# Four attention chains per step, keys paired with forget gates, and a later turn of the first HGRN queries

## The chip, the core and the metric

The kernel runs on one core of a Trainium2 chip. The metric is the device time of one execution in microseconds (us); lower is better. The program uses five engines, each with its own queue that is worked off in order: TensorE (PE in the profile, its weight loads PEld), VectorE (DVE), ScalarE (ACT), GpSimd (POOL) and SyncE (SP, which only issues DMAs). They wait for each other through semaphores.

## The reference, cut to what matters

One layer: a SwiGLU half-step, a token mixer, and a second SwiGLU half-step, each between an RMSNorm on its input and one on its output. 256 tokens, width 2048, all float32. The change lies in the mixer alone:

```python
proj = u @ w_in                                   # 2048 -> 11280 columns
(g_q, g_k, g_v, g_out, g_code, h_q, h_f, h_i, h_out, z_gla, z_hgrn) = split(proj)
gla_log_a = log_sigmoid(g_code @ gla_w_gk_up + gla_b_gk) / 16
o_gla  = rms_norm(gated_attention(g_q, g_k, g_v, gla_log_a)) * silu(g_out)         # 4 heads, keys 128, values 256
log_f  = logaddexp(log(lb), log1p(-lb) + log_sigmoid(h_f));  h_k = -expm1(log_f)
o_hgrn = rms_norm(gated_attention(silu(h_q), h_k, h_i, log_f)) * silu(h_out)       # 8 heads of 128
merged = sigmoid(z_gla + b0) * (o_gla @ w_branch_gla) + sigmoid(z_hgrn + b1) * (o_hgrn @ w_branch_hgrn)
return merged @ w_out
```

`gated_attention` is the causal recurrence S_t = diag(a_t) S_(t-1) + k_t v_t^T, o_t = S_t^T q_t.

## The kernel before, in words

**Wide products.** Tokens stand as two tiles of 128 (t = 0, 1). A float32 operand is split into a high part (rounded on ScalarE, tiles `whi`, `xhi`) and the rest (a subtraction on VectorE, `wlo`, `xlo`), and each product is three matmuls: high x high (L164), low x high (L165), high x low weights (L166). Weights come by DMA into `raw` tiles of a ring with five buffers (`RING`, L31); `split_into` (L157) makes `whi` and `wlo` of them.

**Pairs.** In the mixer, w_in is taken in pairs of blocks of 512 columns (`two`, L1101, which calls `gemm_pair`, L336). A pair runs over eight units of two 128-row tiles. Most units are plain: two steps, one for each block, of 12 matmuls. Three units of a pair (four in later ones) are done with seven products instead of eight (`Blocks.seven`, L272): this needs sums of the weights on VectorE (`wsum`), their high parts on ScalarE (`wsumh`) and rests on VectorE (`wsuml`), and saves an eighth of TensorE's work. A unit with seven products splits its raw tiles as `whi` of L285 (first half), `wsumh` of L287, `whi` of L289 (second half), `wsumh` of L291; the third of its products is the first that reads the half of L289. In a pair with `late=True` the units with seven products come after six plain steps, otherwise after four. At the end of a pair `share` and `close` add up the results in PSUM (`c`, with `psum` in SBUF), and the first steps of the next pair are split ahead (`following`).

**Side work.** Everything else of the mixer is written as generators that `Side` (L48) steps between the steps of wide products. `pump` (L72) steps each light generator once, and then, when it is due and the pair has not come near its units with seven products (`full`), the heavy ones, at most two of them. Light ones turn tiles (`transposed` L814 on TensorE; `turned_into` L823, which copies a tile to 16-bit halves on ScalarE, `halves`, turns it by a DMA that ScalarE issues, and joins it again), make decays (`gla_decays` L1017, `hgrn_gates` L1063) and the diagonal terms (`dots` L854). Heavy ones are the attention chains (`attention` L871): one for each token tile t of the GLA heads, of the first four HGRN heads and of the last four, six in all. A chain waits for its operands, scales the diagonal into `own` (ScalarE, L882), and then goes through seven levels of chunk lengths 1 to 64: small products of keys and queries on TensorE (L899 for the five short levels, 16 products each; L906 for the two long ones), two products of keys and queries with decays on VectorE (L915, L918), a masked copy into `own` (L920) and the decays of the next level (L939). Behind the levels it makes the state and the output (L957 to L969), its norm (squares on ScalarE L975, two steps on GpSimd L397 and L399, a product on VectorE L981), waits two steps, turns the output on TensorE and splits it into `oT`, the operand of the branch products.

**Order of the pairs before.** After the GLA queries and the code block (with the first HGRN queries): GLA keys and first values; second values and first output gates; second output gates and first forget gates; then first HGRN values and output gates; second HGRN queries and forget gates; second HGRN values and output gates; then the branch gates and the branch products. Below, pairs are counted in this order, the first being the one with the GLA keys. The GLA chains step from the third pair on, the first HGRN chains from the fifth, the last ones among the branch products.

**Who sets the order of instructions.** The program's text and the generators give a priority; the scheduler of the tile framework then orders each engine's queue, so that instructions of neighbouring steps interleave.

## Time and profile before

| what | value |
|---|---|
| runs, device time | 2054.09, 2055.51, 2056.26 us (median 2055.51) |
| the profiled execution's own time | 2055.05 us |
| its span, first to last instruction | 2053.3 us |
| granted TensorE clock | 0.999 |
| busy: TensorE, VectorE, ScalarE, GpSimd | 2040.3, 1897.0, 1332.1, 40.1 us |
| second to sixth pair, between VectorE's closing additions | 778.9 to 1013.1 us |

The busy time of TensorE counts a matmul from its start to its modelled end, and neighbours overlap: a 128x512 product shows 0.39 us and starts 0.23 us after the one before. Small gaps show in the starts, not in the share. On the other engines a row of the timeline gives the start, the time to the last end, the engine (a q behind it is its queue), the line, the operation, the tiles written and read, and how many instructions were merged; in brackets stands idle time and what ended it.

### The profile page before, as it was taken

Reading aid. Unit: us, or ns where it says so; the run is one execution under the profiler, and the core shown is the slowest. Engines: PE = TensorE matmul, PEld = TensorE weight load, DVE = VectorE, ACT = ScalarE, POOL = GpSimd, SP = SyncE. Lnnn points to the kernel's source line nnn. Section 1 sums busy time; section 2 is a strip of 40 time slices with the busy share of each in tenths; the row PEclk is TensorE's granted clock in tenths of the full one; section 3 lists DMA queues with packets and bytes.
Section 4 is the critical chain, followed back from the end, with each engine's and each line's share of the span. In section 5 each row is a group of like instructions: output and inputs, shape, how many; then the busy total and the mean of one; then the engine's idle time right before and its main releaser. Section 6 shows DMA issues by size and latency. Waiting matters only on the chain.

```text
span 2053.3 us, 29000 instructions
## 1 busy us (share of the span) xinstructions
PE 2040.3 (99%) x10287; PEld 1695.6 (83%) x10287; DVE 1897.0 (92%) x2237; ACT 1332.1 (65%) x1740; POOL 40.1 (2%) x87
## 2 busy tenths in 40 slices
PE   9999999999999999999999999999999999999998
PEld 8888888888888888878888888889888888888886
DVE  8999999998899879989999898899999999989897
ACT  7666667666666586576655565666666766676663
POOL 1000000000000100000000000010000000000000
PEclk9999999999999999999999999999999999999999
DMA  8777677676757567556566568757767776776664
GB/s 254 228 214 230 202 220 222 214 223 211 224 185 234 163 213 226 164 170 193 172 197 198 180 216 224 237 159 208 244 198 221 221 215 208 222 234 205 204 194 145
DMA packets 256282, 425.60 MB, mean 207 GB/s; under 512 B 72116, under 2 KB 80503, under 8 KB 256136
## 3 DMA queue, kind: packets, MB, share of 16 engines
q1 hardware_dynamic: 196624, 401.80, 61.8%
q10 hardware_dynamic: 59512, 21.94, 5.6%
q8 instruction: 80, 1.31, 0.3%
q14 instruction: 66, 0.54, 0.1%
HBM read 406.11 MB, written 4.19 MB: 200 GB/s over the span
## 4 chain that ended last, share of the span: by engine, by line
PE 91%; DVE 3%; ACT 3%; issue 1%; DMA 1%; POOL 0%; SPq 0%; ACTq 0%; DVEq 0%; POOLq 0%
PE c L164 22%; PE c L166 22%; PE c L165 22%; PE p L166 6%; PE p L164 6%; PE p L165 6%; PE mm L164 2%; PE mm L166 2%; PE mm L165 2%; DVE h L546 1%; PE ps L404 1%; DVE held L160 1%; DMA raw<-in_w_in_dram 1%; DVE wlo L160 0%; PE ps L899 0%
## 5 line engine op out<-in xcount | busy, mean ns | idle before, releaser
L158 ACT ACTIVATE whi<-raw 128x1024 fp32r<-128x1024 f32 (+3 forms) x486 | 491.8, 1025 | 183.7 <-PE c L165 85.8
L160 DVE TENSOR_TENSOR wlo<-raw,whi 128x1024 fp32r<-128x1024 f32 (+3 forms) x486 | 567.9, 1182 | 38.8 <-ACT whi L158 36.6
L164 PE MATMUL c<-whi,xhi 128*128 128x512 f32 (+1 forms) x1350 | 526.1, 390 | 0.5 <-DVE hq L842 0.3
L165 PE MATMUL c<-whi,xlo 128*128 128x512 f32 (+1 forms) x1350 | 522.6, 387 | 0.0
L166 PE MATMUL c<-wlo,xhi 128*128 128x512 f32 (+1 forms) x1350 | 522.4, 387 | 0.3 <-DVE wlo L250 0.3
L250 DVE TENSOR_TENSOR wlo<-raw,whi 128x1024 fp32r<-128x1024 f32 x264 | 313.9, 1218 | 15.7 <-ACT whi L289 12.6
L164 PEld LDWEIGHTS c<-whi,xhi 128*128 128x128 f32 x1350 | 253.4, 188 | 51.9 <-issue 1.1
L166 PEld LDWEIGHTS c<-wlo,xhi 128*128 128x128 f32 x1350 | 253.4, 188 | 51.4 <-DVE wlo L250 0.7
L165 PEld LDWEIGHTS c<-whi,xlo 128*128 128x128 f32 x1350 | 253.5, 188 | 49.3
L289 ACT ACTIVATE whi<-raw 128x1024 fp32r<-128x1024 f32 x132 | 139.5, 1057 | 207.2 <-DVE raw L250 139.8
L250 DVE TENSOR_TENSOR wsuml<-wsum,wsumh 128x1536 fp32r<-128x1536 f32 x132 | 231.1, 1751 | 12.4 <-ACT wsumh L291 12.4
L164 PE MATMUL c<-whi,hkhi 128*128 128x512 f32 x534 | 207.7, 389 | 0.0
L165 PE MATMUL c<-whi,hklo 128*128 128x512 f32 x534 | 207.7, 389 | 0.0
L166 PE MATMUL c<-wlo,hkhi 128*128 128x512 f32 x534 | 207.7, 389 | 0.0
L287 ACT ACTIVATE wsumh<-wsum 128x1024 fp32r<-128x1024 f32 x132 | 138.8, 1052 | 89.5 <-DVE wsum L250 42.8
L285 ACT ACTIVATE whi<-raw 128x1024 fp32r<-128x1024 f32 x132 | 139.1, 1054 | 76.3 <-PE c L165 52.5
L250 DVE TENSOR_TENSOR wsum<-raw,raw 128x1024 f32<-128x1024 f32 x132 | 160.9, 1219 | 21.4 <-DMA raw<-in_ffn_w_down_dram 11.4
L164 PEld LDWEIGHTS c<-whi,hkhi 128*128 128x128 f32 x534 | 100.2, 188 | 21.0
L165 PEld LDWEIGHTS c<-whi,hklo 128*128 128x128 f32 x534 | 100.2, 188 | 20.8
L166 PEld LDWEIGHTS c<-wlo,hkhi 128*128 128x128 f32 x534 | 100.2, 188 | 20.7
L250 DVE TENSOR_TENSOR c<-c,psum 128x512 f32<-128x512 f32 x143 | 94.4, 690 | 8.5 <-PE c L166 8.2
L250 DVE TENSOR_TENSOR wsum<-raw 128x512 f32<-128x512 f32 x132 | 91.1, 690 | 3.8
(347 smaller groups left out, 3072.3 us busy)
## 6 DMA issues: line engine op xcount, KB each, us to landing
raw<-in_ffn_w_down_dram SPq DMA_DIRECT2D x120, 512.0 KB, 4.7
raw<-in_w_in_dram SPq DMA_DIRECT2D x104, 512.0 KB, 4.5
raw<-in_ffn_w_gate_dram SPq DMA_DIRECT2D x90, 512.0 KB, 4.7
raw<-in_ffn_w_up_dram SPq DMA_DIRECT2D x90, 512.0 KB, 3.8
raw<-in_ffn_w_gate_dram SPq DMA_DIRECT2D x140, 256.0 KB, 3.9
raw<-in_ffn_w_up_dram SPq DMA_DIRECT2D x140, 256.0 KB, 4.0
raw<-in_w_in_dram SPq DMA_DIRECT2D x128, 256.0 KB, 3.5
raw<-in_ffn_w_down_dram SPq DMA_DIRECT2D x104, 256.0 KB, 3.8
```

The source lines that it names most:

```text
L158: last[0] = nc.scalar.activation(hi, src, AF.Copy)
L160: nc.vector.tensor_tensor(lo, src, hi.bitcast(F32), op=ALU.subtract)
L164: nc.tensor.matmul(ps, lhsT=xhi, rhs=whi, start=start, stop=False)
L165: nc.tensor.matmul(ps, lhsT=xlo, rhs=whi, start=False, stop=False)
L166: nc.tensor.matmul(ps, lhsT=xhi, rhs=wlo, start=False, stop=stop)
L250: return nc.vector.tensor_tensor(o, x, y, op=op)
L285: nc.scalar.activation(ahi, ra, AF.Copy)
L287: nc.scalar.activation(hi[:, 0:2, :], wsum[:, 0:2, :], AF.Copy)
L289: nc.scalar.activation(bhi, rb, AF.Copy)
L404: end = nc.tensor.transpose(dst_ps[:, i * P:(i + 1) * P], src[:, i * P:(i + 1) * P], ident)
L546: nc.vector.scalar_tensor_tensor(h[t][n], acc[t][n], r1, h[t][n], op0=ALU.mult, op1=ALU.add)
```

## The change

It has six parts. (1) The pairs are put in another order: GLA keys with the first HGRN forget gates; first GLA values with first output gates; second values with second output gates (this one now `late`); the rest as before. So the y tiles, sigmoids and decays of the first HGRN heads, with their diagonal terms, are made behind the first pair instead of the third. (2) The first four chains, two of GLA and two of HGRN, wait for each other (`group`), and from the third pair to the sixth `side.wide` steps up to four chains, every other time that they may step, where before at most two were stepped, in late pairs whenever no light work waited. (3) A chain's start (the copies into `own` and the first product of queries and decays) becomes a light generator, `begin`; `own` has four buffers. (4) A chain's end (turn and split of the output) becomes a light generator, `outputs`, so that the chain is free to go on. (5) The first HGRN queries are turned later: the copy into halves starts 16 and 18 steps after it could, instead of 2 and 4, and is joined after 12 steps instead of 16. (6) Where the first GLA gates go is named by number instead of by count.

No instruction is added or removed on any engine: TensorE has 9683, VectorE 2237, ScalarE 1759 with its DMAs, GpSimd 87, SyncE 1057 in both programs, alike in operation, tiles and shape. Lines of the new kernel are higher, by 5 from `seven` to `transpose4`, by up to 28 further down (L285 becomes L290, L289 L294, L899 L927).

ScalarE, behind the code block, where the GLA decays are made (`e`, `fT`) and the first HGRN queries (`hq`) were turned; before and then now:

```order
L413 ACTIVATE halves_6848<-hq_6403 128x1024
L1093 COPY lcr_6855<-ps_6852 128x512
L428 DMA_TRANSPOSE turned_6850<-halves_6848 128x8x128
L1051 ACT_TABLE_LOAD
L1051 ACTIVATE e_6840<-e_6840 128x512
L413 ACTIVATE halves_6897<-hq_6404 128x1024
L1059 ACT_TABLE_LOAD
L1059 ACTIVATE fT_6401<-m_6842 128x256
L428 DMA_TRANSPOSE turned_6899<-halves_6897 128x8x128
L285 ACTIVATE whi_7000<-raw_6991 128x1024
```

```order
L1110 COPY lcr_6851<-ps_6848 128x512
L1068 ACT_TABLE_LOAD
L1068 ACTIVATE e_6840<-e_6840 128x512
L290 ACTIVATE whi_6992<-raw_6983 128x1024
L1076 ACT_TABLE_LOAD
L1076 ACTIVATE fT_6401<-m_6842 128x256
L292 ACTIVATE wsumh_6986<-wsum_6985 128x1024
```

Both copies into halves and both DMAs have left this place (rows that repeat are left out), and the first split of the unit with seven products stands ahead of the exponentials into `fT`.

ScalarE, at the first unit with seven products of the second pair (`whi_7288` is its first half, `whi_7290` its second; in the new program `whi_7332` and `whi_7334`); before and then now:

```order
L837 ACTIVATE k_7173<-c_1451_6790,r_6194 128x512
L285 ACTIVATE whi_7288<-raw_7279 128x1024
L837 ACTIVATE k_7175<-c_1453_6792,r_6331 128x512
L837 ACTIVATE v_7181<-c_1452_6791,r_6194 128x512
L413 ACTIVATE hqT_6740<-turned_6850 128x2x512
L287 ACTIVATE wsumh_7282<-wsum_7281 128x1024
L289 ACTIVATE whi_7290<-raw_7280 128x1024
L820 COPY kT_7177<-ps_7214 128x512
L882 ACTIVATE own_7230<-diag,gd_7179 128x32 x4
L291 ACTIVATE wsumh_7282<-wsum_7281 128x512
```

```order
L842 ACTIVATE k_7171<-c_1453_6792,r_6331 128x512
L290 ACTIVATE whi_7332<-raw_7323 128x1024
L842 ACTIVATE y_7181<-c_1452_6791,r_6194 128x512
L1190 ACT_TABLE_LOAD
L1190 ACTIVATE hk_7185<-y_7181 128x512
L1085 ACTIVATE hfT_7177<-ps_7207 128x512
L1090 ACTIVATE hfT_7177<-hfT_7177,lb,lc 128x128
L418 ACTIVATE halves_7249<-hq_6404 128x1024
L825 COPY kT_7173<-ps_7253 128x512
L884 ACTIVATE own_7269<-diag,gd_7175 128x32 x4
L292 ACTIVATE wsumh_7326<-wsum_7325 128x1024
L294 ACTIVATE whi_7334<-raw_7324 128x1024
```

Between the two halves of the unit's splits there now stand both y, the table load, both hk, the twenty instructions of both `hgrn_gates` (one of each kind is shown), the second copy into halves with its DMA, both kT and eight copies into `own`; before, one k, both v and one `hqT` stood there.

TensorE, at the first attention level in the third pair; before and then now:

```order
L166 MATMUL c_1618_7555<-wlo_7532,xhi_1328_6155 128x512
L899 MATMUL ps_7570<-qT_6399,kT_7177 32x16 x16
L899 MATMUL ps_7592<-qT_6400,kT_7178 32x16 x16
L164 MATMUL c_1617_7554<-whi_7537,xhi_1313_6060 128x512
L165 MATMUL c_1617_7554<-whi_7537,xlo_1314_6061 128x512
```

```order
L171 MATMUL c_1628_7613<-wlo_7590,xhi_1328_6155 128x512
L927 MATMUL ps_7628<-qT_6399,kT_7173 32x16 x16
L927 MATMUL ps_7650<-qT_6400,kT_7174 32x16 x16
L927 MATMUL ps_7672<-hqT_6740,hkT_7179 32x16 x16
L927 MATMUL ps_7694<-hqT_6741,hkT_7180 32x16 x16
L169 MATMUL c_1627_7612<-whi_7595,xhi_1313_6060 128x512
```

The level's products of four chains stand in one group, and the next group follows after 24 wide products, where a group of two chains followed after 12.

The diff, cut where it only moves text:

```diff
--- before.py
+++ after.py
@@ -57,7 +57,7 @@
     def __init__(self):
         self.light, self.heavy, self.due, self.full = [], [], False, False
-        self.fast = False
+        self.fast = self.wide = False
     def _step(self, queue, g):
         try:
@@ -72,12 +72,17 @@
     def pump(self):
         for g in list(self.light):
             self._step(self.light, g)
-        self.due = not self.light if self.fast else len(self.heavy) < 2 or not self.due
-        if self.due and not self.full:
+        if self.full:
+            return
+        if self.fast and not self.wide:
+            self.due = not self.light
+        else:
+            self.due = len(self.heavy) < 2 or not self.due
+        if self.due:
             steps = 0
             for g in list(self.heavy):
                 steps += self._step(self.heavy, g) != Side.WAITS
-                if steps == 2:
+                if steps == (4 if self.wide else 2):
                     break
     def flush(self):
@@ -842,12 +847,12 @@
                 nc.vector.scalar_tensor_tensor(sg, ps, r, sg, op0=ALU.mult, op1=ALU.mult)
                 return sg
-            def spawn_T(srcs, s, dma=0):
+            def spawn_T(srcs, s, join=0, ahead=0):
                 dsts = []
                 for t, src in enumerate(srcs):
                     dsts.append(blk(s))
-                    side.spawn(turned_into(dsts[-1], src, 2 + 2 * t, dma) if dma else
+                    side.spawn(turned_into(dsts[-1], src, ahead + 2 * t, join) if join else
                                transposed(src, dsts[-1]))
                 return dsts
@@ -868,21 +873,44 @@
                     side.spawn(dots(q, k, d, row))
                 return ds
-            def attention(t, qT, kT, fT, d, vs, gates, dv, br, b0):
-
-
-
-
+            begun = {}
+
+            def begin(qT, kT, fT, d):
                 while not all(id(x) in laid for x in (qT, kT, fT, d)):
-                    yield Side.WAITS
-
-                own = mp.tile([P, 4 * 32], F32, tag="own", name=nm("own"), bufs=2)
+                    yield
+                own = mp.tile([P, 4 * 32], F32, tag="own", name=nm("own"), bufs=4)
                 for i in range(4):
                     nc.scalar.activation(own[:, i * 32:(i + 1) * 32], diag, AF.Copy,
                                          scale=d[:, i:i + 1])
                 nc.vector.tensor_tensor(qT, qT, fT, op=ALU.mult)
-                yield
+                begun[id(qT)] = own
+
+            def outputs(on, key):
+
+                yield
+                yield
+                tp = ps_tile()
+                transpose4(tp, on)
+                hi, lo = [tiles4(blk("oT", F32R)) for _ in range(2)]
+                parts = 2 if key[0] == "g" else 1
+                for k in range(parts):
+                    src, dst, rest = [x[:, k::parts, :] for x in (tiles4(tp), hi, lo)]
+                    w = norms[key[0]][:, k:k + 1]
+                    nc.scalar.activation(dst, src, AF.Copy, scale=w)
+                    nc.vector.scalar_tensor_tensor(rest, src, w, dst.bitcast(F32),
+                                                   op0=ALU.mult, op1=ALU.subtract)
+                oT[key] = hi, lo
+
+            def attention(t, qT, kT, fT, group, vs, gates, dv, br, b0):
+
+
+
+
+
+                while not all(id(x) in begun for x in group):
+                    yield Side.WAITS
+                own = begun[id(qT)]
                 tot, totals, at = fT, blk("tot"), 0
                 for lv, c in enumerate(LEVELS):
                     def halves(x):
@@ -980,19 +1008,8 @@
                         cs = slice(j * dv, (j + 1) * dv)
                         nc.vector.scalar_tensor_tensor(on[:, cs], o[:, cs], r[:, j:j + 1],
                                                        gates[b][t][:, cs], op0=ALU.mult, op1=ALU.mult)
+                    side.spawn(outputs(on, (br, t, b0 + b)))
                     yield
-                    yield
-                    tp = ps_tile()
-                    transpose4(tp, on)
...
-                    oT[br, t, b0 + b] = hi, lo
             def o_lhs(br):
                 def lhs(t, kt):
@@ -1106,7 +1123,7 @@
             qs = [scaled(q[t], rq[t], "q") for t in range(NT)]
-            qT = spawn_T(qs, "qT", 10)
+            qT = spawn_T(qs, "qT", 10, 2)
             fT, hqs = [blk("fT") for _ in range(NT)], [blk("hq") for _ in range(NT)]
             sums = {}
@@ -1117,7 +1134,7 @@
             for t in range(NT):
                 silu(hq0[t][0][:, 16:half], rs[t], hqs[t][:, :half - 16])
                 silu(hq0[t][1][:, :half], rs[t], hqs[t][:, half - 16:])
-            hqT = spawn_T(hqs, "hqT", 16)
+            hqT = spawn_T(hqs, "hqT", 12, 16)
             diag = mp.tile([P, 32], F32, name="diag")
             for r0 in range(0, P, 32):
@@ -1152,29 +1169,17 @@
             nc.vector.tensor_tensor(lc, lc, lm, op=ALU.mult)
             side.spawn(lc_row(0))
-            def attend(qT, kT, fT, dd, dv, br, b0):
+            def attend(qT, kT, fT, dd, dv, br, b0, group):
                 vs, gates = [], []
                 for t in range(NT):
-                    side.heavy.append(attention(t, qT[t], kT[t], fT[t], dd[t], vs, gates, dv, br, b0))
+                    side.spawn(begin(qT[t], kT[t], fT[t], dd[t]))
+                    side.heavy.append(attention(t, qT[t], kT[t], fT[t], group, vs, gates, dv, br, b0))
                 return vs, gates
             for t in range(NT):
                 for n in range(4):
                     nc.sync.dma_start(away[t][n], h[t][n])
-            k, v, ready = two(O_GK, O_GV, (), cols(O_GV + CB), cols(O_GO))
-            ks = [scaled(k[t], rs[t], "k") for t in range(NT)]
-            kT = spawn_T(ks, "kT")
-            dd = spawn_dots(qs, ks, "gd")
-            vs, gates = attend(qT, kT, fT, dd, 256, "g", 0)
-            vs.append([scaled(v[t], rs[t], "v") for t in range(NT)])
-            v, go, ready = two(O_GV + CB, O_GO, ready, cols(O_GO + CB), cols(O_HF))
-            vs.append([scaled(v[t], rs[t], "v") for t in range(NT)])
-            gates.append([silu(go[t], rs[t], h[t][len(gates)]) for t in range(NT)])
-            go, f, ready = two(O_GO + CB, O_HF, ready, cols(O_HI), cols(O_HO), late=True)
-            gates.append([silu(go[t], rs[t], h[t][len(gates)]) for t in range(NT)])
-
-
-            def hgrn(g, qs, qT, f):
+            def hgrn(g, qs, qT, f, group=None):
                 fT, kT = [blk("hfT") for _ in range(NT)], [blk("hkT") for _ in range(NT)]
                 ys, ks = [scaled(f[t], rs[t], "y") for t in range(NT)], []
@@ -1184,7 +1189,7 @@
                     ks.append(blk("hk"))
                     nc.scalar.activation(ks[t], ys[t], AF.Sigmoid, scale=-1.0)
                 dd = spawn_dots(qs, ks, f"hd{g}", lambda g=g: lc_rows[g])
-                return attend(qT, kT, fT, dd, P, "h", g)
+                return attend(qT, kT, fT, dd, P, "h", g, group or qT)
             def values(v, g):
                 return [scaled(v[t], rs[t], "hv", None if g else h[t][2]) for t in range(NT)]
@@ -1193,15 +1198,28 @@
                 return [silu(go[t], rs[t], blk("ho") if g else h[t][3])
                         for t in range(NT)]
-            vs, gates = hgrn(0, hqs, hqT, f)
+            k, f, ready = two(O_GK, O_HF, (), cols(O_GV), cols(O_GO))
+            ks = [scaled(k[t], rs[t], "k") for t in range(NT)]
+            kT = spawn_T(ks, "kT")
+            dd = spawn_dots(qs, ks, "gd")
+            vs, gates = attend(qT, kT, fT, dd, 256, "g", 0, qT + hqT)
+            hvs, hgates = hgrn(0, hqs, hqT, f, qT + hqT)
+            v, go, ready = two(O_GV, O_GO, ready, cols(O_GV + CB), cols(O_GO + CB))
+            side.wide = True
+            vs.append([scaled(v[t], rs[t], "v") for t in range(NT)])
+            gates.append([silu(go[t], rs[t], h[t][0]) for t in range(NT)])
+            v, go, ready = two(O_GV + CB, O_GO + CB, ready, cols(O_HI), cols(O_HO), late=True)
+            vs.append([scaled(v[t], rs[t], "v") for t in range(NT)])
+            gates.append([silu(go[t], rs[t], h[t][1]) for t in range(NT)])
             side.spawn(lc_row(1))
             v, go, ready = two(O_HI, O_HO, ready, cols(O_HQ + CB), cols(O_HF + CB), late=True)
-            vs.append(values(v, 0))
-            gates.append(gates_of(go, 0))
+            hvs.append(values(v, 0))
+            hgates.append(gates_of(go, 0))
             q, f, ready = two(O_HQ + CB, O_HF + CB, ready, cols(O_HI + CB), cols(O_HO + CB), late=True)
             hqs = [silu(q[t], rs[t], blk("hq")) for t in range(NT)]
             vs, gates = hgrn(1, hqs, spawn_T(hqs, "hqT"), f)
             v, go, ready = two(O_HI + CB, O_HO + CB, ready, cols(O_ZG), cols(O_ZG + CB), late=True)
+            side.wide = False
             vs.append(values(v, 1))
             gates.append(gates_of(go, 1))
```

7 lines of the change are left out of this document (removed).

## Prediction

> **What bounds the kernel now.** I read the page first, its row of engine shares.
>
> ```profile
> PE 2040.3 (99%) x10287; PEld 1695.6 (83%) x10287; DVE 1897.0 (92%) x2237; ACT 1332.1 (65%) x1740; POOL 40.1 (2%) x87
> ```
>
> TensorE sets the end, and the change neither adds nor removes an instruction. So the time can move only by gaps in TensorE's stream of wide products, and by what a switch between kinds of products costs. A busy share does not show gaps of tenths of a microsecond; starts do. Then I read the windows of three weight pairs in the mixer (second to fourth; columns: stretch, PE, PEld, DVE, ACT, POOL, clock, DMA).
>
> ```profile
> 778.90:821.30 42.40, 42.40 (x193) 35.20 (x192) 40.69 (x42) 29.15 (x41) 0.00 (x0) 1.00 0.68 213
> 821.30:867.30 46.00, 46.00 (x505) 37.14 (x504) 45.21 (x79) 24.93 (x29) 0.53 (x1) 1.00 0.55 172
> 867.30:919.10 51.80, 51.37 (x268) 40.88 (x267) 45.98 (x59) 41.00 (x87) 3.25 (x5) 1.00 0.55 167
> ```
>
> In the third pair VectorE works 45.2 of 46.0 us. It is a second bound a hair below the first: work brought there has nowhere to go. From the timeline I took for every `wlo` or `wsuml` the **lead**: from its end on VectorE to the first product that reads it. Where the lead is gone, TensorE stands.
>
> ```profile
> 756.39 0.40 PE L165 MATMUL p<-whi,xlo 128*128 128x512 f32 x1
> 757.31 0.50 PE L166 MATMUL p<-wlo,xhi 128*128 128x512 f32 x1 [0.53 <-DVE wlo L250]
> 758.57 0.39 PE L165 MATMUL c<-whi,xlo 128*128 128x512 f32 x1
> 759.21 0.50 PE L166 MATMUL c<-wlo,xhi 128*128 128x512 f32 x1 [0.25 <-DVE wlo L250]
> 855.39 1.75 DVE L250 TENSOR_TENSOR wsuml<-wsum,wsumh 128x1536 fp32r<-128x1536 f32 x1
> 859.35 0.39 PE L166 MATMUL p<-wsuml,xs 128*128 128x512 f32 x1
> 892.74 1.75 DVE L250 TENSOR_TENSOR wsuml<-wsum,wsumh 128x1536 fp32r<-128x1536 f32 x1
> 894.54 0.50 PE L166 MATMUL p<-wsuml,xs 128*128 128x512 f32 x1 [0.43 <-DVE wsuml L250]
> ```
>
> The reader sees two places where TensorE waits (757 to 759, 894) and, between them, a lead of 859.35 - 857.14 = 2.2 us.
>
> **The change part by part.** Back to back, wide products start 0.23 us apart.
>
> *The query turn that goes later.* Two `halves` copies, each with a transposing DMA behind it, stood among the GLA gates' exponentials (the first copy's rows):
>
> ```profile
> 746.64 1.05 ACT L413 ACTIVATE halves<-hq 128x1024 uint16<-128x1024 uint16 x1
> 747.72 1.25 ACTq L428 DMA_TRANSPOSE turned<-halves  x1
> 749.00 1.28 ACT L1051 ACT_TABLE_LOAD   x1 [0.84 <-ACT lcr L1093]
> 754.96 1.05 ACT L285 ACTIVATE whi<-raw 128x1024 fp32r<-128x1024 f32 x1
> ```
>
> Without them ScalarE is 0.95 + 0.84 + 0.95 = 2.7 us earlier (a copy's start to the next start, twice, and the idle time behind the first DMA), and the unit's first `whi` now stands ahead of the fT exponentials. The waits at 757.31 (0.92 instead of 0.23) and 759.21 (0.64) go: 0.7 + 0.4 = 1.1, **-1.2** with a tenth before 756.39. At least 0, at most that.
>
> *Fewer switches.* One group of level products:
>
> ```profile
> 822.86 0.39 PE L166 MATMUL c<-wlo,xhi 128*128 128x512 f32 x1
> 823.18 0.74 PE L899 MATMUL ps<-qT,kT 128*32 128x16 f32 x64
> 823.85 0.49 PE L164 MATMUL c<-whi,xhi 128*128 128x512 f32 x1
> 824.18 0.39 PE L165 MATMUL c<-whi,xlo 128*128 128x512 f32 x1
> ```
>
> 0.32 in and 0.33 out against 0.23, and about a tenth within 0.67: 0.3 us a group. In TensorE's order level products interrupt the wide ones 24 times before and 19 times now; all interruptions together are 55 in both, so five plain transposes, at about 0.1, come instead. -1.5 + 0.5 = **-1.0** (-1.5 to 0).
>
> *The fourth pair's burst.* The decays of the first HGRN heads leave that pair, and with them the wait at 894.54 (0.6) and tenths around it: **-0.8** (0 to -0.9).
>
> *The burst that arrives in the second pair.* The same decays now stand just ahead of that pair's first seven-product unit, which is its fifth unit; in the fourth pair it was the seventh. ScalarE's rows there and the decays' cost:
>
> ```profile
> 777.12 0.69 ACT L837 ACTIVATE k<-c,r 128x512 f32<-128x512 f32 x1 [0.65 <-DVE c L250]
> 778.01 1.06 ACT L285 ACTIVATE whi<-raw 128x1024 fp32r<-128x1024 f32 x1 [0.20 <-PE c L165]
> 779.55 1.25 ACT L837 ACTIVATE v<-c,r 128x512 f32<-128x512 f32 x2
> 782.38 1.06 ACT L287 ACTIVATE wsumh<-wsum 128x1024 fp32r<-128x1024 f32 x1 [0.29 <-DVE wsum L250]
> 783.35 1.04 ACT L289 ACTIVATE whi<-raw 128x1024 fp32r<-128x1024 f32 x1
> 786.46 1.79 ACT L882 ACTIVATE own<-diag,gd 128x32 f32<-128x32 f32 x8
> 868.50 1.14 ACT L1185 ACTIVATE hk<-y 128x512 f32<-128x512 f32 x2
> 870.72 0.58 ACT L1068 ACTIVATE hfT<-ps 128x512 f32<-128x512 f32 x1
> 878.05 0.58 ACT L1093 COPY lcr<-ps 128x512 f32<-128x512 f32 x1
> ```
>
> Before, the unit's second `whi` (L289) ends at 784.4. Now the order is k, whi, k, whi (L285), ending 3.0 us after 777.1, at 780.1; then without a split between: y twice 1.2, table load 1.3, hk twice 1.1, the 20 instructions of the decays 7.3 (870.72 to 878.05), `halves` 1.0, kT twice 1.0 (128x512, of y's form, without its scale), own eight times 1.7, `wsumh` 1.0, and that `whi` 1.0. Sum 16.6: it ends at 796.7. Its first reader, at 791.12, among its neighbours:
>
> ```profile
> 784.14 1.29 DVE L859 TENSOR_TENSOR k<-q,k 128x512 f32<-128x512 f32 x2 [0.41 <-PE ps L404]
> 788.81 1.75 DVE L250 TENSOR_TENSOR wsuml<-wsum,wsumh 128x1536 fp32r<-128x1536 f32 x1
> 791.12 0.39 PE L164 MATMUL c<-whi,xhi 128*128 128x512 f32 x1
> 791.58 0.39 PE L166 MATMUL c<-wlo,xhi 128*128 128x512 f32 x1
> 792.94 0.39 PE L166 MATMUL p<-wsuml,xs 128*128 128x512 f32 x1
> 783.44 1.03 PE L404 MATMUL ps<-ident,k 128*128 128x128 f32 x8
> ```
>
> TensorE came there at 791.12; eight transposes of y come first (0.9, like those of k) and 0.3 of waiting for y: 792.3. It stands 4.4 us. Then `wlo` is 1.2 behind its `whi` where the reader is 0.46 behind: 0.7 more; `wsuml`, 1.7 on VectorE, costs 0.3. With y's 0.3: **+5.7**. Behind the waiting product the whole queue of TensorE waits; the ring is five chunks deep and refills only as chunks are read. Low end 2.5, if the y and hk copies start some 2 us earlier and small copies run into each other; high end 6.9, if the second `halves`' DMA blocks ScalarE for 1.25, as at 747.72. I take 5.7, from the rows of like form.
>
> The Trainium skill, page "ScalarE: Activation LUTs", section "What ACT_TABLE_LOAD costs", gives 1.28 us for the load and about as much again for a drain before it; here the row has 1.28 and the next copy starts at once. By the page's sum the term would be some 1.4 us larger; the row decides.
>
> *VectorE in the third and fourth pair.* Ahead of the second pair's first `wsuml` come four hk products and two reductions, six full-width passes at 0.60 like the two at 784.14: 3.6 us. Waiting for the burst, that `wsuml` ends with no lead, where it had 2.4 (788.81 + 1.75 to 792.94). From there to the third pair's last `wsuml` VectorE gets two query products (1.2) and 12 chain steps instead of 10: each two products of 128x256 at 0.33 behind one another (0.42 alone, row at 834.59), a masked copy near 0.2 and sums of decays near 0.3, by the same width. With sums for four chains taken ahead, 4.8 us more. TensorE reads that one 1.6 us later in its stream. Lead there: 2.2 - 2.4 - 4.8 + 1.6 = -3.4. VectorE's idle time that came only from waiting can be won back:
>
> ```profile
> 811.28 1.22 DVE L160 TENSOR_TENSOR wlo<-raw,whi 128x1024 fp32r<-128x1024 f32 x1 [0.73 <-ACT whi L158]
> 834.59 0.42 DVE L915 TENSOR_TENSOR kT<-kT,tot 128x256 f32<-128x256 f32 x1 [0.59 <-PE ps L899]
> 886.12 1.22 DVE L250 TENSOR_TENSOR wlo<-raw,whi 128x1024 fp32r<-128x1024 f32 x1 [2.58 <-ACT whi L285]
> 889.34 0.88 DVE L981 SCALAR_TENSOR_TENSOR on<-ps,r,h 128x256 f32<-128x256 f32 x2 [2.00 <-POOL r L399]
> ```
>
> With 1.6 of it, -1.8. At the fourth pair (894.54) the same sum is 0.1 - 2.4 - 2.9 - 3.3 = -8.5, against 7.3 of idle: -1.2. These are one debt, not two: **+2.0**, from 0 to 5 (half the idle not won back).
>
> *The outputs.* In the sixth pair six groups of `on` transposes stand 1 to 6 us behind their products, where before they stood 5 to 36; the way between is square, two POOL steps, product, and the row at 889.34 shows 2.0 us of waiting for POOL alone. **+1.0** (0 to 3). What leaves the later pairs buys nothing: the last wait of TensorE over half a microsecond in the mixer's pairs is the one at 894.54. The weight loads on SP's queue keep size and number, only their columns change, and the DMA share of 0.55 to 0.68 in the windows leaves them room: nothing.
>
> Sum: -1.2 - 1.0 - 0.8 + 5.7 + 2.0 + 1.0 = +5.7. On the profiled execution's own 2055.05 (span 2053.3, 1.75 around it) that is 2060.75; the median of the runs, 2055.51, lies 0.5 above it, so I say **2061**.
>
> **The rivals.**
>
> *The burst is covered.* ScalarE is 65% busy, and in the fourth pair the same decays cost under 1 us. If small copies overlap and the chunks split ahead carry TensorE, the +5.7 shrinks to about 2.6 and VectorE gets that time back: -3.0 + 2.6 + 0 to 1 = 2055.5, no change. Against it: in the fourth pair six plain units and two groups of attention stood in front.
>
> *The idle pays for all.* Decays covered entirely, VectorE's 7.3 us of idle absorbs the debt, waits gone: 2055.5 - 3.0 = 2052.5, and 2051 with the last waits elsewhere. For it: 886 to 892 is 5.2 us of avoidable waiting. Against it: that idle comes after the place that stalls.
>
> *The clock falls.* TensorE starts slow in this trace:
>
> ```profile
> L1330 PE MATMUL ps<-idle 128*128 128x512 f32 x11 | 4.5, 561 | 1.3 <-POOL idle L1325 1.3
> ```
>
> Eleven fillers after the start take 561 ns against 389. If a stall of 4 us puts it back there, one such stretch costs 11 x 0.17 = 1.9: 2063, and with the debt's high end 2066. Against it: the clock is 1.00 in every window above, but no gap there reaches 1 us. The Trainium skill, page "TensorE: Matmul & The Clock Gate", section "Part 1: The HAM clock gate", says that an idle window of about 3.4 us halves the clock until about as long has been busy; by that rule a gap of 4.4 us is just enough, if it meets the window.
>
> That the chains do not step together is ruled out by the order of instructions, where all four stand in one group.
>
> **How the numbers follow.** This kernel's measurement tells 0.2%, 4.1 us, from no change: slower begins at 2059.6, faster at 2051.4. Forecast 50%, own range 2057 to 2065, seven tenths of it slower; covered burst 25%, no change; idle pays 12%, under half of it faster; clock 13%, slower. Slower 0.35 + 0.13 = 0.48 and a little for the debt alone, 0.49; faster 0.05; same 0.46. The range leaves out the fastest and slowest tenth: 2053 to 2067.
>
> **What would show it.** Right: in the second pair's fifth unit a gap of about 4 us before a `c<-whi` product, released by `whi` L294 (the new line of L289), with ScalarE busy without a split for 13 us or more; no waits at 757 and 759; deferred `wsuml` in the third pair with leads near 0. Wrong: no gap over 2 us in the second pair (the burst is hidden), or larger gaps at the sixth pair's `on` transposes than there.

## The result: 12 us slower

The changed kernel takes 2067.53 us (median of 6 runs, 2066.95 to 2068.69), the one before 2055.19 (6 runs, 2053.92 to 2056.26). The ratio is 1.0061, 95% interval 1.0051 to 1.0072: slower, and by more than the 2061 that was forecast; the range, up to 2067, ends 0.5 us short of it. The profiled execution's span is 2066.2 us, 12.9 more than before.

The place is the mixer's ten pairs. First the windows from the first pair's last sum to the mixer's end, of the kernel before and of the changed one with its second, third, fourth and sixth pair (stretch, PE, PEld, DVE, ACT, POOL, clock, DMA; the stretch's ends are the closing sums on VectorE).

```profile
778.90:1239.20 460.30, 459.87 (x3109) 377.10 (x3107) 432.90 (x581) 288.21 (x451) 13.07 (x22) 1.00 0.61 189
```

```profile
780.70:1253.10 472.40, 463.97 (x3103) 378.54 (x3104) 432.76 (x581) 288.69 (x452) 16.01 (x22) 0.99 0.59 184
780.70:830.30 49.60, 45.41 (x191) 36.81 (x192) 41.42 (x48) 40.30 (x72) 2.10 (x4) 0.93 0.54 163
830.30:879.30 49.00, 49.00 (x581) 40.17 (x580) 48.97 (x95) 23.23 (x27) 0.00 (x0) 1.00 0.55 173
879.30:925.50 46.20, 46.15 (x473) 36.64 (x474) 44.58 (x68) 29.67 (x49) 0.00 (x0) 1.00 0.59 183
970.70:1032.40 61.70, 59.38 (x293) 48.29 (x292) 50.42 (x70) 45.49 (x105) 10.57 (x13) 1.00 0.47 145
```

VectorE does the same work in both, 432.9 and 432.8 us, in 12.1 us more of time. The second pair went from 42.4 to 49.6 with 8.2 us in which VectorE stands; in the third, 46.0 before and 49.0 now, VectorE is busy to the last tenth. The fourth gives 5.6 back (51.8 before), and the sixth takes 61.7 where it took 47.7. The pairs do not hold the same side work in both kernels, because the chains' steps and ends stand elsewhere, so a longer pair is not yet a price; only the whole is. The clock column says 0.93 in the second pair.

What TensorE waits for in the whole of the changed kernel, the waits over half a microsecond that the mixer holds:

```profile
PE c L169 <- ACT whi L294: 3.5, 1, 3.5
PE ps L409 <- DVE on L1009: 2.0, 3, 0.8
PE ps L409 <- ACT y L842: 1.9, 1, 1.9
...
PE mm L171 <- DVE wlo L165: 1.2, 1, 1.2
PE c L169 <- ACT sc L961: 0.7, 1, 0.7
PE c L171 <- DVE wlo L255: 0.5, 1, 0.5
```

The waits of before at 757.31, 759.21 and 894.54 are gone. The two largest new ones stand in the second pair, on TensorE's timeline (start, duration, instruction; in brackets the idle time ahead and its releaser):

```profile
778.55 0.39 PE L171 MATMUL c<-wlo,xhi 128*128 128x512 f32 x1
780.83 1.42 PE L409 MATMUL ps<-ident,y 128*128 128x128 f32 x8 [1.89 <-ACT y L842]
...
782.48 0.63 PE L170 MATMUL c<-whi,xlo 128*128 128x512 f32 x1
782.90 0.63 PE L171 MATMUL c<-wlo,xhi 128*128 128x512 f32 x1
...
793.76 0.39 PE L171 MATMUL c<-wlo,xs 128*128 128x512 f32 x1
797.68 0.50 PE L169 MATMUL c<-whi,xhi 128*128 128x512 f32 x1 [3.53 <-ACT whi L294]
798.94 0.80 PE L171 MATMUL c<-wlo,xhi 128*128 128x512 f32 x1 [0.53 <-DVE wlo L255]
799.53 0.63 PE L169 MATMUL p<-whi,xs 128*128 128x512 f32 x1
799.96 0.63 PE L170 MATMUL p<-whi,xs 128*128 128x512 f32 x1
```

From the last product before it to the next, less 0.23, TensorE stands 2.05 us for y and 3.69 for `whi`. Behind both, products start 0.43 us apart instead of 0.23 for about three microseconds. The reason for the second wait is ScalarE's row of small work, as forecast:

```profile
780.09 1.28 ACT L842 ACTIVATE y<-c,r 128x512 f32<-128x512 f32 x2 [0.18 <-DVE c L255]
781.39 1.28 ACT L1190 ACT_TABLE_LOAD   x1
782.69 1.15 ACT L1190 ACTIVATE hk<-y 128x512 f32<-128x512 f32 x2
...
791.08 1.05 ACT L418 ACTIVATE halves<-hq 128x1024 uint16<-128x1024 uint16 x1
792.02 0.57 ACT L825 COPY kT<-ps 128x512 f32<-128x512 f32 x1
792.16 1.25 ACTq L433 DMA_TRANSPOSE turned<-halves  x1
793.45 0.59 ACT L825 COPY kT<-ps 128x512 f32<-128x512 f32 x1 [0.85 <-PE c L171]
793.93 1.80 ACT L884 ACTIVATE own<-diag,gd 128x32 f32<-128x32 f32 x8
795.64 1.04 ACT L292 ACTIVATE wsumh<-wsum 128x1024 fp32r<-128x1024 f32 x1
796.58 1.04 ACT L294 ACTIVATE whi<-raw 128x1024 fp32r<-128x1024 f32 x1
```

Behind it VectorE stands too, for twice as long as TensorE: with the reductions done, the next on its queue is the `wlo` of that `whi`, and nothing behind it runs first:

```profile
797.66 1.23 DVE L255 TENSOR_TENSOR wlo<-raw,whi 128x1024 fp32r<-128x1024 f32 x1 [7.08 <-ACT whi L294]
798.80 1.75 DVE L255 TENSOR_TENSOR wsuml<-wsum,wsumh 128x1536 fp32r<-128x1536 f32 x1
```

### The profile page after: what moved, and what is told of

The parts are those of the page before. It is cut to its first block, busy times and chain, and to the rows that moved or that the text cites. A ratio compares the mean times of both kernels' runs of the same rounds, so it can differ in the third digit from the quotient of the medians.

```text
span 2066.2 us, 28980 instructions
## 1 busy us (share of the span) xinstructions
PE 2045.1 (99%) x10287; PEld 1698.8 (82%) x10287; DVE 1897.6 (92%) x2237; ACT 1331.3 (64%) x1740; POOL 42.9 (2%) x87
## 4 chain that ended last, share of the span: by engine, by line
PE 90%; DVE 4%; ACT 3%; issue 2%; DMA 1%; POOL 1%; ACTq 0%; DVEq 0%; POOLq 0%
PE c L169 21%; PE c L171 21%; PE c L170 21%; PE p L169 6%; PE p L170 6%; PE p L171 6%; PE mm L171 2%; PE mm L169 2%; PE mm L170 2%; DVE h L551 1%; DVE wlo L165 1%; ACT whi L163 1%; PE ps L409 1%; DMA raw<-in_w_in_dram 1%; DVE held L165 0%
## 5 line engine op out<-in xcount | busy, mean ns | idle before, releaser
L163 ACT ACTIVATE whi<-raw 128x1024 fp32r<-128x1024 f32 (+3 forms) x486 | 491.2, 1025 | 174.6 <-PE c L170 73.6
L294 ACT ACTIVATE whi<-raw 128x1024 fp32r<-128x1024 f32 x132 | 139.4, 1056 | 186.6 <-DVE raw L255 125.5
L255 DVE TENSOR_TENSOR wsuml<-wsum,wsumh 128x1536 fp32r<-128x1536 f32 x132 | 231.2, 1751 | 14.8 <-ACT wsumh L296 14.8
L290 ACT ACTIVATE whi<-raw 128x1024 fp32r<-128x1024 f32 x132 | 139.0, 1053 | 72.6 <-PE c L170 52.1
```

The lines of the kernel that those rows point to most:

```text
L163: last[0] = nc.scalar.activation(hi, src, AF.Copy)
L255: return nc.vector.tensor_tensor(o, x, y, op=op)
L290: nc.scalar.activation(ahi, ra, AF.Copy)
L294: nc.scalar.activation(bhi, rb, AF.Copy)
```

## The experiments

Below, the burst is the row of small ScalarE work for the first HGRN heads that now stands in the second pair. Two theories were to be told apart: A, that TensorE's stalls behind the burst (and the slow products after them) are the cost; B, that VectorE's work in the second and third pair sets the time, and the stalls matter through it. Each kernel is the changed one with the edit shown, unless it says otherwise. Medians of 4 to 11 runs; the kernel before, run beside them, had 2054.7 to 2055.0.

### The burst, moved (gates8)

```
 def hgrn_gates(y, t, g, fT, kT):
-    yield
+    for _ in range(1 if g else 8): yield
```

> The decays of the first HGRN heads (transposes of y, and the 20 copies on ScalarE behind them) start seven side steps later, behind the second pair's seven-product units. Theory A (the burst stalls TensorE, and each stall also costs clock): in the changed kernel TensorE stands 2.05 us at 780.83 for y and 3.69 at 797.68 for the second whi of the unit, 0.5 more for its wlo, and after each stall some 8 wide products start 0.43 instead of 0.23 us apart, 1.8 us each. All of that goes, -2.0 -3.7 -0.5 -3.6 = -9.8, and the copies cost up to 2 in their new place: 2057.7 to 2059.7, with the clock at 1.00 in all of the second pair. Theory B (VectorE's debt is the bound, the stalls only give it time): without the stalls VectorE, which stood 7.1 us in the second pair, comes late in the third, and at least half comes back: 2062 to 2065, with waits for wsuml between 830 and 880.

2062.96 us, ratio to before 1.0039 (1.0026 to 1.0051): 4.6 less than the changed kernel, about half of what A asked and inside B's range. The windows of the second and third pair:

```profile
779.90:822.30 42.40, 40.69 (x186) 32.81 (x185) 40.35 (x45) 36.08 (x67) 2.10 (x4) 1.00 0.63 192
822.30:872.90 50.60, 49.74 (x580) 39.97 (x579) 50.43 (x99) 26.99 (x32) 0.00 (x0) 1.00 0.54 167
```

The second pair is back at 42.4, and its clock at 1.00. But the third grew by 1.6, filled with VectorE's work (50.4 of 50.6). The waits for `wsuml` that B named are not there; instead TensorE stands 0.9 us at 844.67 for a `whi` of L294, because ScalarE had stood 13.5 us for the `wsum` that VectorE makes. The stall was real, and part of it only moved the debt.

### Two chains at a time (nowide), and both edits (nowide_gates8)

```
-            side.wide = True
+            side.wide = False
```

> The new order of pairs stays, but the chains are stepped two at a time all through, as before the change. Theory A (the new order brings the burst, and that costs most): nothing changes up to the second pair's end, so the waits for y and for the second whi and the slow products behind them stay, and so does their cost of some 9 us; of what comes later (waits for `on` 3.1, for sc 0.9, for wlo at 1081 1.4) a part goes: 2062 to 2067. Rival (stepping the chains together is what costs, by the work on VectorE in the third pair): 2055 to 2058.

> New order of pairs, chains two at a time, and the decays behind the second pair's seven-product units: the edits of nowide and gates8 together. If the burst and the stepping together cost apart from each other, the gains add: 2067.5 - 3.3 - 4.6 = 2059.6, from 2058.5 to 2060.7. If the stall only gave VectorE time that it needs anyway in the third pair, less than half of the 4.6 is left beside nowide's 2064.3: 2062 or more.

nowide: 2064.26 (ratio 1.0045, 1.0031 to 1.0058), 3.3 less. nowide_gates8: 2056.27 (1.0006, 0.9997 to 1.0015), 11.3 less than the changed kernel and no longer told from the kernel before. So the gains did not merely add (2059.6 was expected): late decays are worth 8.0 with two chains at a time and 4.6 with four; stepping together costs 3.3 beside the burst and 6.7 without it. Second and third pair of nowide:

```profile
780.70:830.70 50.00, 44.65 (x191) 36.11 (x192) 41.44 (x48) 40.33 (x72) 1.05 (x2) 0.93 0.54 162
830.70:877.30 46.60, 46.60 (x507) 37.61 (x507) 46.07 (x79) 22.52 (x26) 0.00 (x0) 1.00 0.61 181
```

and of nowide_gates8:

```profile
781.00:823.40 42.40, 40.60 (x186) 32.73 (x185) 40.34 (x45) 36.02 (x67) 1.05 (x2) 1.00 0.63 192
823.40:870.90 47.50, 47.50 (x511) 38.41 (x510) 47.22 (x80) 27.12 (x33) 0.00 (x0) 1.00 0.58 177
```

Over both pairs together, the time split into VectorE's work and the time it stands (any stretch can be split so; the point is what each column depends on), and the time from the same start to the fourth pair's end and to the mixer's end:

| kernel | both pairs | VectorE's work | VectorE stands | to the fourth pair's end | to the mixer's end |
|---|---|---|---|---|---|
| before | 88.4 | 85.9 | 2.5 | 140.2 | 460.3 |
| changed | 98.6 | 90.4 | 8.2 | 144.8 | 472.4 |
| nowide | 96.6 | 87.5 | 9.1 | 147.7 | 468.5 |
| gates8 | 93.0 | 90.8 | 2.2 | 139.1 | 466.7 |
| nowide_gates8 | 89.9 | 87.6 | 2.3 | 140.3 | 460.4 |

In the four kernels with the new order VectorE stands 0.5 us or less in the third pair; the burst sets the column "VectorE stands", the number of chains stepped there the one before it (90.4 to 90.8 with four, 87.5 with two). But that is work brought forward, on TensorE too (x581 and x580 instructions in the third pair with four chains, x507 and x511 with two), and the fourth pair gives it back. The fourth pair of gates8, then the fourth and the sixth of nowide_gates8:

```profile
872.90:919.00 46.10, 46.10 (x476) 36.61 (x476) 44.57 (x66) 29.96 (x49) 0.00 (x0) 1.00 0.60 184
870.90:921.30 50.40, 49.44 (x292) 39.96 (x291) 45.30 (x66) 32.63 (x60) 2.64 (x4) 1.00 0.57 173
968.50:1015.90 47.40, 47.29 (x400) 38.37 (x399) 46.52 (x66) 37.74 (x72) 1.00 (x2) 1.00 0.56 168
```

At the fourth pair's end the kernels with four chains are ahead of those with two, by 2.9 and 1.2 us. At the mixer's end they are behind, by 3.9 and 6.3. What stepping together costs therefore shows behind the fourth pair. The sixth is the longest of those with four chains (61.7 in the changed kernel and in gates8); it holds the waits for `on`, but also work that stands elsewhere with two.

### Where stepping together costs (g8o4_widelater, g8o4_three)

Both have late decays and late outputs (next section). Then g8o4_widelater steps four chains only from the fourth pair on, and g8o4_three takes three:

```
 v, go, ready = two(O_GV, O_GO, ready, cols(O_GV + CB), cols(O_GO + CB))
-side.wide = True
...
 v, go, ready = two(O_GV + CB, O_GO + CB, ready, cols(O_HI), cols(O_HO), late=True)
+side.wide = True
```

```
-                if steps == (4 if self.wide else 2):
+                if steps == (3 if self.wide else 2):
```

> Late decays, outputs after four side steps, and the chains stepped two at a time in the third pair, four together only from the fourth on. If VectorE's crowd in the third pair is what stepping together costs (50.5 of 50.6 us there, 47.4 of 47.5 in nowide_gates8): most of the 4.2 between gates8_outs4 (2060.5) and nowide_gates8 (2056.3) goes: 2056.5 to 2058.5. If the cost is in the pairs behind it (waits for sc, oT and wlo between 921 and 1072): 2059.5 to 2061.

> Late decays, outputs after four side steps, and three chains' steps taken together instead of four. If the cost goes by how much VectorE work falls into the third pair, it lies between two (2056.3) and four (2060.5): 2057.5 to 2059.5. If only the number of switches counts, it is no faster than four: 2060 to 2061.

2057.31 (1.0013, 1.0003 to 1.0023) and 2058.71 (1.0021, 1.0012 to 1.0031), against 2060.46 with four from the third pair on: both inside the ranges that the third pair's crowd asked for. With two chains there and four afterwards, the third pair takes 47.5, as in nowide_gates8. But g8o4_three has no crowd there either, and is 1.4 slower:

```profile
822.00:869.70 47.70, 47.70 (x481) 38.59 (x481) 47.17 (x84) 27.50 (x34) 0.00 (x0) 1.00 0.56 177
```

So the third pair's crowd is not shown to be the cost. Both edits also move the chains' steps and ends in all the pairs behind it, and no run holds those still.

### The outputs (outs4, gates8_outs4)

```
 def outputs(on, key):
-    yield
-    yield
+    for _ in range(4):
+        yield
```

> Each output waits four side steps instead of two before it is transposed. Theory A: the waits of TensorE for `on` in the sixth pair (0.4 + 0.7 + 0.9 + 0.3 + 0.9 = 3.1 us between 987 and 1008) go, -3.1, or -1.5 where the transposes still meet them: 2064.4 to 2066.0. Rival: TensorE is ahead there only because the work behind is late anyway, and the same time comes back as waits for wlo in the pairs behind: 2067 to 2068.

> The late decays of gates8 and the outputs that wait four side steps. In the trace of outs4 the stretch from the second pair's end to the end of the mixer's branches is 2.0 us shorter than in the changed kernel. If the waits for `on` are real cost there: 2063.0 - 2.0 = 2061.0. If they come back elsewhere: 2062.5 to 2063.5.

Alone 2067.34 (1.0055, 1.0041 to 1.0068), nothing by the medians, although the three waits for `on` left the list of waits (0.2 us of them stays): its runs lie from 2065.0 to 2068.7, and the profiled one had 5.3 us of standing for `whi` where the changed kernel had 3.7. Without the burst the effect is plain: 2060.46 (1.0026, 1.0016 to 1.0037), 2.5 less than gates8, of which 2.0 were expected.

### The later turn alone (before_turn, before_turn_again), and the old order of pairs (pairs_back)

The kernel before, with the turn as the change has it (`spawn_T` given its `ahead`):

```
-            hqT = spawn_T(hqs, "hqT", 16)
+            hqT = spawn_T(hqs, "hqT", 12, 16)
```

> The kernel before with only the later turn of the first HGRN queries. By the rows of both traces the waits at 757.31 and 759.21 go (0.7 + 0.4) and nothing else moves: 2055.2 - 1.2 = 2054.0. Rival: the two copies and their transposing DMAs fall into the first pair's end and cost as much there: 2055 to 2056.

> The kernel before with only the later turn of the first HGRN queries, once more, since its interval (0.9985 to 1.0003) did not tell a gain of 1 us from none. By the waits that left the trace: 2053.8, a ratio of 0.9994 to 0.9996 with the interval below 1. If the 0.9 us were chance: 2054.5 to 2055.5.

2053.84 and, run again, 2053.47, beside 2054.78 and 2054.88: 0.9 and 1.4 less, both times with a ratio of 0.9994 and an interval of 0.9985 to 1.0003. The waits at 757 and 759 are gone from its trace. It is the fastest kernel of this study, but a gain of 1 us stays below what the interval tells.

pairs_back is the changed kernel with the old order of pairs and no stepping together:

```
-            k, f, ready = two(O_GK, O_HF, (), cols(O_GV), cols(O_GO))
+            k, v, ready = two(O_GK, O_GV, (), cols(O_GV + CB), cols(O_GO))
...
-            vs, gates = attend(qT, kT, fT, dd, 256, "g", 0, qT + hqT)
+            vs, gates = attend(qT, kT, fT, dd, 256, "g", 0, qT)
```

> The pairs stand in the order of before again and each group of two chains waits for its own alone; the later turn, the new start of a chain and the outputs as side steps of their own stay. Theory A: without the new order there is no burst in the second pair, and the time is that of before with the later turn (2053.8), within 1.5: 2052.5 to 2055.5. Rival (the outputs and starts as steps of their own cost by themselves): 2057 or more.

2057.90 (1.0015, 1.0006 to 1.0024), from 2055.8 to 2060.8: a miss, at the time that the rival gave (starts and outputs as steps of their own). There is no burst, but one new wait, on TensorE:

```profile
785.09 0.45 PE L927 MATMUL ps<-qT,kT 128*32 128x16 f32 x32 [2.80 <-ACT kT L825]
```

With its start a step of its own and no second group to wait for, the first chain's level products are placed in the second pair, just behind kT, whose copies stand behind a split and a transposing DMA on ScalarE. The waits in the changed kernel (`group`) happen to keep them out of there. The trace is of the fastest run, 2055.8; what the median adds to it is not shown, and the rival is not ruled out.

### The clock (fill)

```
-            self.product((0, 0), self.lhs(0, k0 + 1), second[1])
+            for _ in range(side.idle): nc.tensor.transpose(self.p["p6"][:, :P], ident, ident)
+            side.idle = 0; self.product((0, 0), self.lhs(0, k0 + 1), second[1])
...
-                transpose4(tp, y)
+                for _ in range(18 if (t, g) == (0, 0) else 0): nc.tensor.transpose(tp[:, :P], ident, ident)
+                side.idle = 0 if g else 30; transpose4(tp, y)
```

> The two stalls stay, but TensorE is kept busy in them: 18 transposes of the identity ahead of those of y and 30 ahead of the product that waits for the second whi, into tiles that are overwritten. Theory A (the clock falls because TensorE stands): the wide products behind both places stay 0.23 us apart, -1.8 twice: 2063.9, with the waits for y and whi ending where they did. If only the stall itself is lost and the slow products have another cause (what ScalarE, VectorE or the transfers do at the time), they stay 0.43 apart: 2067.5, or up to 1 more if the transposes run over the end of a stall.

TensorE's timeline of fill at the first place and the next wait:

```profile
778.76 2.12 PE L1084 MATMUL ps<-ident 128*128 128x128 f32 x18
780.73 1.04 PE L410 MATMUL ps<-ident,y 128*128 128x128 f32 x8
781.83 0.39 PE L170 MATMUL c<-whi,xlo 128*128 128x512 f32 x1
782.06 0.40 PE L171 MATMUL c<-wlo,xhi 128*128 128x512 f32 x1
...
798.98 0.50 PE L171 MATMUL p<-wsuml,xs 128*128 128x512 f32 x1 [1.64 <-DVE wsuml L255]
```

With TensorE busy, no product in the second pair starts 0.43 from the next: the slow products come from standing. The medians do not follow: 2067.89 (1.0063, 1.0050 to 1.0075), from 2066.05 to 2070.37. The experiment is not clean, since the 48 transposes also moved two splits ahead of the burst on ScalarE. In the profiled execution TensorE waits 1.6 us for `wsuml` instead, still reads it 2.7 us earlier than the changed kernel (798.98, 801.66), and ends the mixer 2.2 us earlier; behind the mixer 1.7 of that is lost in a stretch that the change does not touch (44.8 us from 1340.3 on, 43.1 from 1342.5 in the changed kernel). So these few runs do not settle a gain of one or two microseconds. In the changed kernel `wsuml` was ready at 798.80 + 1.75 = 800.55 and read at 801.66: with ScalarE and VectorE as they were, some 1.1 us of the second slow stretch could have been won there. The first slow stretch costs nothing, as nowide shows, which had none there:

```profile
780.86 1.26 PE L409 MATMUL ps<-ident,y 128*128 128x128 f32 x8 [1.76 <-ACT y L842]
781.87 0.47 PE L169 MATMUL c<-whi,xhi 128*128 128x512 f32 x1
782.19 0.39 PE L170 MATMUL c<-whi,xlo 128*128 128x512 f32 x1
...
797.73 0.80 PE L169 MATMUL c<-whi,xhi 128*128 128x512 f32 x1 [5.16 <-ACT whi L294]
```

It came to the same product 1.6 us earlier, at full clock, waited that much longer, and went on at 797.73 instead of 797.68.

### Shortening the stall without VectorE's part (halves_late, late2, gates8_drop)

Of halves_late, late2 and, on top of gates8, gates8_drop (which leaves out the products of the first HGRN diagonal, so that its output is not the reference's):

```
-                    side.spawn(turned_into(dsts[-1], src, ahead + 2 * t, join) if join else
+                    side.spawn(turned_into(dsts[-1], src, ahead + (14 if ahead > 9 else 2) * t, join - (10 * t if ahead > 9 else 0)) if join else
```

```
-v, go, ready = two(O_GV, O_GO, ready, cols(O_GV + CB), cols(O_GO + CB))
+v, go, ready = two(O_GV, O_GO, ready, cols(O_GV + CB), cols(O_GO + CB), late=True)
```

```
-    nc.vector.tensor_tensor(k, q, k, op=ALU.mult)
-    if row is not None:
+    if row is None or 1 in lc_rows: nc.vector.tensor_tensor(k, q, k, op=ALU.mult)
+    if row is not None and 1 in lc_rows:
         nc.vector.tensor_tensor(k, k, row(), op=ALU.mult)
```

> The second tile of the first HGRN queries is copied and turned some twelve side steps later, behind the second pair's units: one copy of 128x1024 (0.95) and the 0.85 that ScalarE stood behind its transposing DMA leave the burst. Theory A (what counts is when ScalarE's row of copies ends): the second whi ends 1.8 earlier and TensorE waits 1.9 instead of 3.7: 2065.7. If the DMA's hold does not delay what is behind it: 2066.6. If the time at the second pair's end is VectorE's, not ScalarE's: 2067.5.

> The second pair has its seven-product units two plain units later (as the fourth has them), nothing else: the burst stays where it is on ScalarE, but 24 more wide products (24 x 0.227 = 5.4 us) stand ahead of the first that needs the second whi. Theory A: the waits there (3.7 and 0.5) and the slow products behind go, the wait for y stays: 2067.5 - 4.2 - 1.1 = 2062.2, from 2061 to 2063.5. Rival: the five chunks of the ring run dry instead, since a plain chunk's split now stands behind the burst: a wait for a whi of L163 in its place, 2066 to 2068.

> The decays start behind the second pair's seven-product units, as in gates8, and the four products on VectorE for the first HGRN diagonal (query times key, times the row of lc: 4 x 0.60 = 2.4 us) are left out, so the HGRN output is not the reference's. Theory B (what is left in gates8 is VectorE's debt): its waits for wlo at 790.15 (1.1) and for wsuml at 792.42 (0.6) go, -1.7 to -2.4 against gates8: 2060.5 to 2061.3. If VectorE's debt is not what TensorE waits for, nothing moves: 2063.

halves_late: 2068.80 (1.0067, 1.0053 to 1.0082); late2: 2068.25 (1.0066, 1.0052 to 1.0081). Both shortened the second pair's stall, and no gain shows in the medians. The windows of late2, and TensorE's waits for VectorE in its third pair:

```profile
780.40:828.00 47.60, 46.18 (x253) 37.37 (x256) 40.53 (x45) 40.09 (x71) 2.08 (x4) 0.96 0.57 171
828.00:878.30 50.30, 47.99 (x539) 38.27 (x529) 49.83 (x99) 23.68 (x28) 0.00 (x0) 1.00 0.54 168
PE c L171 <- DVE wlo L165: 1.7, 3, 0.7
```

TensorE stands 1.4 us for a `whi` there (of L163, as the rival had it) instead of 3.7; the second pair is 2.0 shorter and the third 1.3 longer, at 49.8 of 50.3 on VectorE; VectorE's standing over both fell by 0.7 only. In halves_late ScalarE's row ends 1.9 earlier (15.65 us behind the start of y instead of 17.53), the second pair is 1.7 shorter, and the third takes 51.2. This is theory B at work: in the changed kernel TensorE has no such wait in the third pair; in late2 it waits there three times for a `wlo` of VectorE (1.7 us), in halves_late once (0.7), and once more for a `whi` (0.6 in each). So most of what is won in the second pair comes back in the third. The four runs of each spread over 2.0 and 2.8 us, and in the traces the mixer ends 0.7 and 1.5 us earlier than in the changed kernel; a gain of about a microsecond is not excluded, the forecast 5.3 of late2 is.

gates8_drop: 2062.34 (1.0037, 1.0023 to 1.0051), 0.6 less than gates8 for 2.4 us of work left out. It does not decide what it was made for: ScalarE's splits were put in another order, the second `whi` came behind `own`, and TensorE waited 1.2 us at 789.69 for that `whi` and 0.5 for its `wlo`, with VectorE idle for 2.2 us ahead of the `wlo`.

## Why the prediction missed: the right place, the wrong price

The place was the right one: the burst on ScalarE in the second pair, in the unit and at the product that were named, with the debt on VectorE in the third pair behind it (there the deferred `wsuml` end 0.3 us ahead of their first reader in the changed kernel, 2.2 to 2.6 before). The time is 6.5 us above the forecast. What failed is the price: burst and stepping together were put at 5.7 + 2.0 + 1.0 = 8.7, and taking both out (nowide_gates8) gives back 11.3. Term by term:

- **The later query turn, -1.2.** Right in size for itself (-0.9 and -1.4 in the kernel before, not told from zero). In the changed kernel it should buy nothing: the waiting product hangs on ScalarE's row, and a TensorE that comes earlier waits longer. No run of the changed kernel without the turn shows this.
- **Fewer switches, -1.0.** No such gain is seen. Adding up what TensorE's starts lie later than back to back, below 0.24 us each, between the first pair's closing and the mixer's end gives 14.8 us before and, without the two slow stretches, some 15.5 now.
- **The fourth pair's burst, -0.8.** Its wait left, but one of 0.94 came at 928.25 (for `sc`, ScalarE again; it is gone in nowide).
- **The burst, +5.7.** This term was mis-sized. ScalarE's row was right to a tenth up to the second kT: the second `whi` was put at 796.7 and ended at 797.62, and 0.85 of that is the hold behind the transposing DMA, which I had seen at 747.72 and left to the high end. The table load took its 1.28 us with no drain on either side (the copy ahead ends at 781.37, the next starts at 782.69). TensorE's stall for `whi` is 3.7 (4.4 forecast), that for y 2.05 (0.3 forecast). What failed is the step "It stands 4.4 us", taken for the price: it counts from an arrival at 791.12 in the kernel before, with a wait of 0.3 for y. The product that waits stands 16.98 us behind the first pair's closing sum (797.68 - 780.70), and 8.54 behind it where the burst is moved away (gates8, 788.44 - 779.90): it comes 8.4 later, where the forecast had 5.6 (791.12 to 796.7). The runs say that moving the burst away is worth 8.0 with two chains at a time (nowide to nowide_gates8) and 4.6 with four; in the traces the third pair takes 0.9 of it back with two and 1.6 with four, and the rest of that difference stays open. In nowide_gates8 that unit still waits 1.35 and 0.77 us for `wlo` and `wsuml`, behind VectorE's new work; counted with the burst, which no run shows apart, it is 10.1.
- **What the gains left.** nowide_gates8 is 1.4 us above the kernel before (2056.3 to 2054.9 beside it) with those 2.1 and a wait of 1.1 for `oT` at 899 in it. So of the forecast gains some 1.8 are there, as much as the turn and the fourth pair's wait were to bring; the fewer switches cannot be among them, since this kernel steps two chains. This is a sum, not a run of its own.
- **VectorE in the third and fourth pair, +2.0 (0 to 5), and the outputs, +1.0 (0 to 3).** The outputs cost 2.5 (gates8_outs4), inside their bounds. Both together, by nowide, cost 3.3 beside the burst, near the 3.0 forecast, but 6.7 without it; the first agreement is luck, as the two costs were added as if they stood apart. That the fourth pair's idle time pays the third pair's debt came true: with four chains the fourth pair ends 2.9 and 1.2 us ahead of two chains. What the prediction left out is that the cost of stepping together shows behind the fourth pair. Of the 6.7 the outputs' 2.5 are shown; g8o4_widelater saves 3.1 more; which wait these stand for stays open.
- **The rivals.** That the burst is covered, or that idle time pays for all, fell with the first row of the second pair. That the clock falls came true, at both stalls of the profiled execution, and yet is not where most of the 6.5 us are: the first stretch is waited for anyway, the second is worth some 1.1.

What stays open, besides the place of the stepping's cost: the share of the clock in single runs. pairs_back's runs spread over 5 us, and whether a slow stretch behind its wait of 2.8 us makes the difference could only be seen in the runs that were not profiled.

## What to carry to other kernels

A stall is not priced by the wait that is seen, but by how much later the waiting product comes than it would without the cause, and by what the stretch behind it can take back. Here TensorE stood 3.7 us, the product came 8.4 us later, and moving the cause away gained 4.6 to 8.0; edits that shortened only the stall moved most of it into waits in the next pair, where VectorE was full. Before work is brought into a stretch, read the second-busiest engine's row there: at 45.2 of 46.0 us each microsecond brought makes that stretch one longer. Whether the kernel is longer shows only where the work was taken from: here the fourth pair gave it back, and the cost of stepping together came later. And of two waits in a row on one engine only the last counts if what ends it did not depend on the first, as with ScalarE's row here; terms are then summed along the chain that ends last, not over all waits.

## What the runs showed that was not expected

The clock falls after a shorter gap than thought, and not each time. Of the gaps between products in the second pair, 2.05 (changed kernel) and 2.16 us (late2) were followed by products 0.43 us apart; 1.80 (fill), 1.93 (nowide), 2.29 (outs4) and 2.97 (pairs_back) were not; 3.42 (halves_late), 3.69 (changed kernel), 5.30 (outs4) and 5.32 (nowide) all were, and none of 1.4 or less. The slow stretches last about 3 us. The Trainium skill, page "TensorE: Matmul & The Clock Gate", section "Part 1: The HAM clock gate", has a window of about 3.4 us that runs free of the kernel. That a gap of 2.05 meets it and one of 2.97 does not agrees with this; but the page puts the slow state behind an idle window of full length, and here 2.05 us were enough.

A transposing DMA that ScalarE issues holds it back: behind the row at 792.16 (1.25 us on its queue) the engine stands 0.85 ahead of the second kT (in gates8, behind the same DMA at 784.03, 0.37). The row names a product as releaser, but in halves_late, where that DMA is gone from there, the same two copies run without a gap:

```profile
790.03 1.06 ACT L825 COPY kT<-ps 128x512 f32<-128x512 f32 x2
790.97 1.82 ACT L884 ACTIVATE own<-diag,gd 128x32 f32<-128x32 f32 x8
```
